# Holding decays, block-sum stores and row squares to the source's order, and loading x a step ahead, in a hybrid SSD and gated-linear-attention layer

## The chip, the cores and the metric

One core of one Trainium2 chip runs the kernel. The metric is the device time in microseconds of one execution. Three executions of the kernel before took 2349.11, 2349.48 and 2352.76 us; the median is 2349.48 us. Traces come from one further execution under the hardware profiler.

## The reference

One layer over 2048 tokens with 16 meta tokens in front, model width 1024, all in float32. `u` is the RMS-normed input; one projection of it gives the inputs of two branches, whose outputs are projected, gated and merged:

```python
def hybrid_layer(hres, norm_w, w_in, ...):
    u = rmsnorm(hres, norm_w)
    proj = jnp.einsum('bld,dn->bln', u, w_in)
    z, xbc, dt_raw, q, k, v, g_gla, a_lr, merge_g = split_cols(proj, IN_WIDTHS)
    xbc = jax.nn.silu(causal_depthwise_conv(xbc, conv_w, conv_b))
    ...
    y_m, s_m = ssd_chunked(xs[:, :m], dt[:, :m], a, bm[:, :m], cm[:, :m], N_META, s0)
    y_r, _ = ssd_chunked(xs[:, m:], dt[:, m:], a, bm[:, m:], cm[:, m:], SSD_CHUNK, s_m)
    ...
    o_r, _ = gla_chunked(q[:, m:], k[:, m:], v[:, m:], log_a[:, m:], GLA_CHUNK, st_m)
    ...
    branch_proj = jnp.einsum('blnc,ncd->blnd', branches, w_branch)
    gates = jax.nn.sigmoid(merge_g.reshape(b, l, N_BRANCH, D_MODEL))
    merged = jnp.sum(gates * branch_proj, axis=2)
    return hres + jnp.einsum('bld,de->ble', merged, w_out)
```

The final result is the RMS norm of this, without the meta rows. In the SSD branch `decay = exp(where(causal, seg, -inf))` with `seg` the differences of the running sums of `dt * a` in a chunk of 128 tokens; the meta tokens are a chunk of their own whose final state starts the first real chunk.

## The kernel before

**Two phases.** The first (to about 1557 us of the trace) does the norm, the input projection of both branches and the two scans; it leaves the branches' outputs and `u` in HBM. The second does the merge gates, the branch projections and the output projection as three kinds of stage with fast matrix multiplication (seven products in place of eight), whose sums of blocks of the right-hand side are needed beforehand. Every float32 product is three products of split operands: `accum` (L181) multiplies high by high (L183), high by low (L184) and low by high (L185).

**Blocks, groups, steps.** The first phase runs over four blocks of 512 tokens. A block has four SSD groups (`ssd_proj`, L448) and then four GLA heads (`gla_proj`, L602), the SSD half and the GLA half of the block. Each is a generator that yields after a *tile* of projection work: a group in the middle of and after its z tile and after each of four feature tiles (x, x, B, C); a head after q, k, the middle and the end of v and two gate tiles. That is six steps each. After every yield, `step()` (L813) moves every running background generator on by one piece, in the order in which they began: scans of earlier groups and heads (`ssd_scan`, `gla_scan`), the GLA gates (`gates`), the next block's `u` (`load_u` by way of `fetch_u`), and the block sums (`beside_unit`). So the source's order is tile, pieces of the others, tile, and so on.

**What is held to it.** TensorE's and SyncE's instructions are kept in source order (`manual_schedule` at L826). ScalarE, VectorE and GpSimd are ordered when the program is built, by a planner that takes an instruction as soon as it holds its inputs to be there; among those ready, the one earlier in the source comes first. So on these engines an instruction can stand far ahead of its place in the source. Once built, each engine runs its list in order and waits at each instruction until its inputs and buffers are there; this holds for DMA issues too, on SyncE (the sync queue) and on ScalarE.

**Buffers.** Weights land in "whl" (four buffers, two loads to a tile; `load_w` at L155). In block 0 they come as one float32 tile through "wr" (three buffers) and are split by ScalarE (L163) and GpSimd (L164), and the split pair is kept in HBM (L179); blocks 1 to 3 load the pair itself (L159). A feature tile's conv accumulator is in "acc" (two buffers, freed by L481), its result in "act" (eight). After the matmuls of a feature tile, ScalarE copies and scales it (L472, L473), VectorE adds three taps (L477), ScalarE takes a tanh (L480) and VectorE finishes silu (L481).

**Block sums.** `make_sums` (L72) runs for one unit in three steps: four loads into two "wr" buffers (L76); four subtractions on GpSimd (L80); two stores from ScalarE's queue (L83). `beside_unit` (L820) runs eight units one after the other, three steps each, so one run of eight fills one half of a block. It is begun at both halves of blocks 1 and 2 and at the first half of block 3: 40 units. The other units run in the second phase, from another pool.

**The next block's u.** `load_u` begins with the GLA half of the block before. For each of four chunks of 128 rows it loads the rows in two halves into "acc" (L256), squares and sums them on ScalarE (L257) and makes the reciprocal root; then TensorE spreads the roots (L278), and for each of eight column tiles of the transposed x it loads the tile into "acc" (L292), multiplies (L294), splits it (L296, L298) and stores it from ScalarE's queue (L297). Each chunk and each column is one step.

**The SSD scan.** `before(c)` transposes chunk c (L538), copies B (L547) and makes the decays: four Relu (L550) on `cb`, a broadcast row fetched by DMA (L490), one Exp (L552), times the masked scores (L553). `after(c)` multiplies (L562 to L565) and sums the squares of a row (L577). In block 0, `meta_state` (L513) multiplies and copies the meta tokens' state (L517), from which `after(0)` reads (L563).

**Late constants.** `late_constants` (L330) loads the gates' second weight and the masks; its first tile, `w2r`, is an "acc" buffer. It is called between block 0's first and second group.

Of the kernel before, what the change touches and what calls it, by code (L numbers as in the profile page):

```python
# [14 lines left out]
P = 128  # L15
# [25 lines left out]
def trunk_kernel(ctx: ExitStack, tc: tile.TileContext, xm, xmt, w_feat, w_tok, w_zm, w_br, w_o,  # L41
# [27 lines left out]
    UNIT = 2 * BLK  # L69
    nsb = seq // UNIT  # L70

    def make_sums(pool, tag, nb, braw, sums, j, c, store):  # L72
        cs = slice(c * HB, (c + 1) * HB)
        pair = [mk(pool, [P, 512], F32, tag, bufs=nb).rearrange("p (i c) -> p i c", i=2) for _ in range(2)]
        for r, (k, t) in zip((t[:, i] for t in pair for i in range(2)), ((0, 1), (0, 0), (1, 1), (1, 0))):
            nc.sync.dma_start(r, braw(4 * k + j, t)[:, cs])  # L76
        yield
        (b12, b11), (b22, b21) = [(t[:, 0], t[:, 1]) for t in pair]
        for o, x, y in ((b11, b12, b11), (b12, b22, b12), (b22, b22, b11), (b21, b21, b22)):
            nc.gpsimd.tensor_tensor(o, x, y, op=ALU.subtract)  # L80
        yield
        for dst, src in zip(sums, pair):
            store.dma_start(dst[j][:, :, cs], src)  # L83

    def new_sums(name):
        return [[wdram.tile([P, 2, BLK], F32, tag=f"{name}_t{i}_{j}", name=f"{name}_t{i}_{j}", bufs=1)
# [132 lines left out]
    def halves_of(pool, tag):  # L219

        bks = [bank(pool, tag) for _ in range(2)]
        return bks, [(i // 2, bks[i // 2][:, i % 2 * 256:(i % 2 + 1) * 256]) for i in range(4)]

    def rstd_of(ssq, n, scale):
        r = mk(sm, [P, 4], F32, "rstd")
        nc.vector.tensor_scalar(r[:, :n], ssq, scale, EPS, op0=ALU.mult, op1=ALU.add)
        nc.gpsimd.tensor_tensor(r[:, :n], r[:, :n], mhalf[:, :n], op=ALU.pow)
        return r
# [6 lines left out]
    def load_u(b):  # L235
        m0 = META if b == 0 else 0
        row0 = META - m0 + b * BLK
        tt = m0 + BLK
        pair = mk(upool, [P, 2, KT * (META + BLK)], F32R, "u")[:, :, :KT * tt]
        uh, ul = [pair[:, i].rearrange("p (k t) -> p k t", k=KT) for i in range(2)]  # L240

        def rows_rstd(r0, n, vector=False):
            ss = mk(sm, [P, 1], F32, "ss")
            if m0:
                xt = mk(wk, [P, D], F32, "tok4", bufs=NT4)
                nc.sync.dma_start(xt[:n], xm[r0:r0 + n, :])
                if vector:
                    nc.vector.scalar_tensor_tensor(xt[:n], xt[:n], 1.0, xt[:n], op0=ALU.mult, op1=ALU.mult,
                                                   accum_out=ss[:n])
                else:  # L250
                    nc.scalar.activation(xt[:n], xt[:n], AF.Square, accum_out=ss[:n])
            else:
                s2 = mk(sm, [P, 2], F32, "ss2")
                for i in range(2):
                    xt = mk(wk, [P, META + BLK], F32, "acc")[:, :BLK]
                    nc.sync.dma_start(xt, xm[r0:r0 + n, i * BLK:(i + 1) * BLK])  # L256
                    nc.scalar.activation(xt, xt, AF.Square, accum_out=s2[:, i:i + 1])  # L257
                nc.vector.tensor_tensor(ss, s2[:, 0:1], s2[:, 1:2], op=ALU.add)
            r = mk(sm, [P, 1], F32, "rs1")
            nc.vector.tensor_scalar(r[:n], ss[:n], 1.0 / D, EPS, op0=ALU.mult, op1=ALU.add)  # L260
            nc.gpsimd.tensor_tensor(r[:n], r[:n], mhalf[:n, 0:1], op=ALU.pow)
            return r

        rs = []
        if m0:
            rm_s = rows_rstd(0, META, True)
        for c in range(NCH):
            rs.append(rows_rstd(META + b * BLK + c * P, P, c % 2))
            yield
        if m0:  # L270
            rs.append(rm_s)
            nc.sync.dma_start(cst[:, :2], cf32[:, :2])
            nc.sync.dma_start(pv, pvec)
            for q in range(NWR):
                raws[f"zm_{q}"] = load_raw(w_zm[:, q * 288:(q + 1) * 288])
        rb = bank(pt, "pt")
        for c in range(NCH):
            nc.tensor.matmul(rb[:, c * P:(c + 1) * P], rs[c].to_broadcast([P, P]), ident, start=True, stop=True)  # L278
        rbs = [(rb, m0, BLK)]
        if m0:  # L280
            rm = bank(pt, "pt")
            nc.tensor.matmul(rm[:, :META], rs[NCH][:META].to_broadcast([META, P]), ident[:META, :META],
                             start=True, stop=True)
            rbs = [(rm, 0, META)] + rbs
        else:
            rbc = mk(wk, [P, 3 + META + BLK], F32, "cin")[:, :BLK]
            nc.scalar.activation(rbc, rb, AF.Copy)
            rbs = [(rbc, 0, BLK)]
            yield
        for kt in range(KT):  # L290
            xk = mk(wk, [P, META + BLK], F32, "act" if m0 else "acc", bufs=NACT if m0 else 2)[:, :tt]
            nc.sync.dma_start(xk, xmt[:, kt, row0:row0 + tt])  # L292
            for ps, a, n in rbs:
                nc.vector.scalar_tensor_tensor(xk[:, a:a + n], xk[:, a:a + n], norm_w[:, kt:kt + 1], ps[:, :n],  # L294
                                               op0=ALU.mult, op1=ALU.mult)
            nc.scalar.activation(uh[:, kt, :tt], xk, AF.Copy)  # L296
            nc.scalar.dma_start(u_left[b][kt], xk[:, m0:])  # L297
            nc.vector.tensor_tensor(ul[:, kt, :tt], xk, uh[:, kt, :tt].bitcast(F32), op=ALU.subtract)  # L298
            yield
        return uh, ul  # L300

# [26 lines left out]
    msk = const.tile([P, NMSK, P], U8, name="msk")  # L328

    def late_constants():  # L330
        w2r = mk(wk, [P, META + BLK], F32, "acc")[:48, :512]
        for i in range(3):
            nc.sync.dma_start(w2r[16 * i:16 * i + 16, :], gw2)
        nc.scalar.activation(w2, w2r, AF.Copy)
        nc.vector.tensor_tensor(w2[32:48], w2r[32:48], w2[32:48].bitcast(F32), op=ALU.subtract)
        mstg = mk(wk, [P, D], F32, "tok4", bufs=NT4)[:, :NMSK * P]
        nc.sync.dma_start(mstg, cmsk)
        nc.vector.tensor_copy(msk.rearrange("p l t -> p (l t)"), mstg)
# [153 lines left out]
    def ssd_scan(o, g, feats, zs):  # L492
# [37 lines left out]
        def before(c):  # L530
            a = m0 + c * P
            ci = ci0 + c
            if c + 1 < NCH:
                fetch_cb(o, g, c + 1)
            cb = cbs.pop((g, c))
            ps = bank(pt, "pt")
            for j, f in enumerate((x0, x1, bf)):
                nc.tensor.transpose(ps[:, j * P:(j + 1) * P], f[:, a:a + P], ident)  # L538
            px = ps[:, :256].rearrange("p (h c) -> p h c", c=64)
            xdt = mk(wk, [P, 4, 64], F32, "c1", bufs=NC1)  # L540
            nc.vector.tensor_tensor(xdt, px, hb(tkd[:, ci, hs], P), op=ALU.mult)
            xw = mk(wk, [P, 4, 64], F32, "c1", bufs=NC1)
            nc.vector.tensor_tensor(xw, px, hb(wde[:, ci, hs], P), op=ALU.mult)
            nc.vector.tensor_tensor(yt[:, c].rearrange("p (h c) -> p h c", c=64), px,
                                    hb(d_skip[:, hs], P), op=ALU.mult)
            bt = mk(wk, [P, P], F32, "bt")
            nc.scalar.activation(bt, ps[:, 256:384], AF.Copy)  # L547
            dm = mk(wk, [P, 4, P], F32, "sq", bufs=NSQ)
            for h in range(4):
                nc.scalar.activation(dm[:, h], cb[:, h], AF.Relu, scale=-1.0,  # L550
                                     bias=tkc[:, ci, 4 * g + h:4 * g + h + 1])
            nc.scalar.activation(dm, dm, AF.Exp, scale=-1.0)  # L552
            nc.vector.tensor_tensor(dm, dm, scm[:, c].unsqueeze(1).to_broadcast([P, 4, P]), op=ALU.mult)  # L553
            held[c] = xdt, xw, bt, dm

# [24 lines left out]
        yield  # L580
        if m0:
            meta_state()
        for c in range(1, NCH):
            before(c)
            after(c - 1)
            yield
# [233 lines left out]
    def beside_unit(key):  # L820
        for j in range(4):
            for c in range(2):
                yield from make_sums(wpool, "wr", NWR, *sums[key], j, c, nc.scalar)
                yield

    with tc.manual_schedule(engines={mybir.EngineType.PE, mybir.EngineType.SP}):  # L826
        for b in range(nblk):
            o = new_block(b, next_u[b])
            for i in range(SG + GH):
                if (b, i) in beside:  # L830
                    begin(beside_unit(beside[b, i]))
                if (b, i) == (0, 1):
                    late_constants()
                if i == 1:
                    begin(gates(o))
                if i == SG and b + 1 < nblk:
                    begin(fetch_u(b + 1))
                for _ in ssd_proj(o, i) if i < SG else gla_proj(o, i - SG):
                    step()
            save(0)  # L840
        while running or begun:
            step()
# [329 lines left out]
```

## Time and profile before

| | |
|---|---|
| median of three runs | 2349.48 us |
| the profiled execution | 2353.29 us |
| its span | 2351.5 us |
| mean granted TensorE clock | 0.982 |
| POOL wr L80 waiting for loads (wr<-y, wr<-u, wr<-in_w_o) | 172.7, 160.7, 68.8 us |
| SPq L159 waiting for PE pj L185 (weight buffers coming free) | 610.2 us, 188 times |

The span is the time from the first to the last instruction. PE is TensorE, PEld its weight loads, DVE VectorE, ACT ScalarE, POOL GpSimd, SP SyncE; SPq, ACTq and DVEq are the engines' instruction queues, in which DMA issues stand. L numbers are lines of the kernel before. In a row of waits, "PE pj L183 <- ACT whl L163: 10.1, 2, 6.7" reads: before the instruction at L183 that writes `pj`, PE was idle until ACT's L163 (writing `whl`) had ended, 10.1 us in total, twice, at most 6.7. In a timeline row the first number is the start, the second the duration (of a merged run, x and a count), and the bracket at the end the idle time before it and what ended it. In the list of DMA issues the last number is the median time in us from issue to landing.

### The profile page before, as it was taken

The numbers are of one execution on the slowest core, as the hardware profiler recorded it, in microseconds if no ns is written. First come the engines' busy times: TensorE is split into PE (matmuls) and PEld (weight loads), VectorE is DVE, ScalarE is ACT, GpSimd is POOL, SyncE is SP. The second block draws the span as 40 slices with busy tenths as digits, with TensorE's granted clock in tenths as the row PEclk, the third lists the DMA queues.
The fourth block names the chain that finished last, engine by engine and source line by source line (L and its number), as shares of the span: only waits on it lengthen the run. The fifth ranks groups of instructions, "written<-read, shape, count | busy, mean of one in ns | idle before, by whom it ended". The sixth has DMA issues, their size and how long they took to land.

```text
span 2351.5 us, 36473 instructions
## 1 busy us (share of the span) xinstructions
PE 2251.0 (96%) x12641; PEld 1962.2 (83%) x12641; DVE 1547.5 (66%) x2895; ACT 1181.6 (50%) x2758; POOL 672.9 (29%) x681
## 2 busy tenths in 40 slices
PE   7799999999999999999999999879999999999998
PEld 7689889889888988888988898768878788888786
DVE  5576665676675567566568655674578854778866
ACT  5565655465534455543456443464455454554543
POOL 4343433122321212221122200207423354423331
PEclk9899999999999999999999999989999999999999
DMA  7665875666786676777677654447577876777753
GB/s 270 225 206 184 299 252 193 204 218 223 240 274 191 205 223 219 238 258 224 194 225 221 205 174 157 154 135 254 194 242 261 297 236 203 251 272 252 254 165 122
DMA packets 301545, 518.05 MB, mean 220 GB/s; under 512 B 27696, under 2 KB 143664, under 8 KB 301360
## 3 DMA queue, kind: packets, MB, share of 16 engines
q1 hardware_dynamic: 200400, 402.84, 52.9%
q10 hardware_dynamic: 100960, 112.88, 13.8%
q8 instruction: 99, 1.62, 0.3%
q14 instruction: 86, 0.70, 0.1%
HBM read 368.42 MB, written 147.19 MB: 219 GB/s over the span
## 4 chain that ended last, share of the span: by engine, by line
PE 48%; DMA 6%; DVE 6%; ACT 3%; issue 2%; SPq 1%; POOL 1%; ACTq 0%; DVEq 0%; POOLq 0%
PE pj L183 6%; PE pj L185 6%; PE pj L184 6%; PE psa L183 4%; PE psa L185 4%; PE psa L184 4%; PE psb L184 2%; PE psb L185 2%; PE psb L183 2%; DVE b L893 1%; DMA br<-br_t 1%; PE psc L183 1%; PE psc L185 1%; PE psc L184 1%; PE pc L562 1%
## 5 line engine op out<-in xcount | busy, mean ns | idle before, releaser
L183 PE MATMUL pj<-u,whl 128*128 128x512 f32 (+1 forms) x1184 | 447.9, 378 | 10.5 <-ACT whl L163 3.5
L185 PE MATMUL pj<-u,whl 128*128 128x512 f32 (+1 forms) x1184 | 431.8, 365 | 0.8 <-POOL whl L164 0.8
L184 PE MATMUL pj<-u,whl 128*128 128x512 f32 (+1 forms) x1184 | 430.8, 364 | 0.0
L183 PE MATMUL pj<-whl,u 128*128 128x256 f32 (+1 forms) x992 | 290.3, 293 | 8.2 <-ACT whl L163 6.7
L185 PE MATMUL pj<-whl,u 128*128 128x256 f32 (+1 forms) x992 | 283.4, 286 | 1.5 <-DVE u L298 1.4
L184 PE MATMUL pj<-whl,u 128*128 128x256 f32 (+1 forms) x992 | 283.4, 286 | 1.0 <-POOL whl L164 1.0
L183 PEld LDWEIGHTS pj<-u,whl 128*128 128x128 f32 x1184 | 225.9, 191 | 48.8 <-ACT whl L163 3.9
L183 PE MATMUL psa<-b,a 128*128 128x512 f32 x640 | 249.8, 394 | 11.1 <-ACT sn L930 8.2
L185 PEld LDWEIGHTS pj<-u,whl 128*128 128x128 f32 x1184 | 224.9, 190 | 36.9 <-POOL whl L164 1.1
L184 PEld LDWEIGHTS pj<-u,whl 128*128 128x128 f32 x1184 | 225.5, 190 | 33.6
L185 PE MATMUL psa<-b,a 128*128 128x512 f32 x640 | 251.3, 393 | 1.2 <-DVE a L914 1.2
L184 PE MATMUL psa<-b,a 128*128 128x512 f32 x640 | 251.0, 392 | 0.0
L183 PEld LDWEIGHTS pj<-whl,u 128*128 128x128 f32 x992 | 191.2, 193 | 9.4 <-ACT whl L163 6.9
L184 PEld LDWEIGHTS pj<-whl,u 128*128 128x128 f32 x992 | 191.0, 193 | 2.1 <-POOL whl L164 1.6
L185 PEld LDWEIGHTS pj<-whl,u 128*128 128x128 f32 x992 | 190.8, 192 | 2.2 <-DVE u L298 2.2
L893 DVE TENSOR_TENSOR b<-br,b 128x512 fp32r<-128x512 f32 x196 | 153.1, 804 | 56.2 <-ACT b L892 55.7
L80 POOL TENSOR_TENSOR wr<-wr 128x256 f32<-128x256 f32 x80 | 65.1, 814 | 425.5 <-DMA wr<-y 169.7
L904 POOL TENSOR_TENSOR as<-ar,ar 128x512 f32<-128x512 f32 x40 | 57.8, 1446 | 447.5 <-DMA ar<-in_w_br 191.2
L164 POOL TENSOR_TENSOR whl<-wr,whl 128x512 fp32r<-128x512 f32 (+1 forms) x100 | 132.9, 1335 | 182.5 <-ACT whl L163 155.2
L892 ACT ACTIVATE b<-br 128x512 fp32r<-128x512 f32 x196 | 119.2, 626 | 112.3 <-DMA br<-br_t 41.5
L914 DVE TENSOR_TENSOR a<-ar,a 128x512 fp32r<-128x512 f32 x160 | 131.8, 839 | 64.4 <-ACT a L913 64.1
L477 DVE SCALAR_TENSOR_TENSOR acc<-cin,hcw,acc 128x512 f32<-128x512 f32 (+1 forms) x192 | 154.6, 805 | 27.0 <-ACT acc L473 26.3
(271 smaller groups left out, 5062.7 us busy)
## 6 DMA issues: line engine op xcount, KB each, us to landing
whl<-k_s SPq DMA_DIRECT2D x96, 512.0 KB, 4.5
whl<-k_g SPq DMA_DIRECT2D x96, 512.0 KB, 4.2
whl<-k_v SPq DMA_DIRECT2D x48, 512.0 KB, 3.7
whl<-k_z SPq DMA_DIRECT2D x36, 512.0 KB, 3.8
wr<-in_w_feat SPq DMA_DIRECT2D x64, 256.0 KB, 4.2
k_s<-whl SPq DMA_DIRECT2D x32, 512.0 KB, 3.7
cb<-cumd ACTq DMA_DIRECT2D x64, 256.0 KB, 5.4
y<-gg ACTq DMA_DIRECT2D x64, 256.0 KB, 4.5
```

Of the source, the lines that this page charges most:

```text
L80: nc.gpsimd.tensor_tensor(o, x, y, op=ALU.subtract)
L164: nc.gpsimd.tensor_tensor(hl[:, 1], raw, hl[:, 0].bitcast(F32), op=ALU.subtract)
L183: nc.tensor.matmul(ps, sh, mh, start=first, stop=False, **kw)
L184: nc.tensor.matmul(ps, sh, ml, start=False, stop=False, **kw)
L185: nc.tensor.matmul(ps, sl, mh, start=False, stop=last, **kw)
L477: nc.vector.scalar_tensor_tensor(acc, cin[:, k:k + tt], hcw[:, ti, k:k + 1], acc, op0=ALU.mult, op1=ALU.add)
L562: nc.tensor.matmul(py[:, h * 64:(h + 1) * 64], dm[:, h], xdt[:, h], start=True, stop=True)
L892: nc.scalar.activation(t[:, 0], raw, AF.Copy)
L893: nc.vector.tensor_tensor(t[:, 1], raw, t[:, 0].bitcast(F32), op=ALU.subtract)
L904: nc.gpsimd.tensor_tensor(s1, a21, a22, op=ALU.add)
L914: nc.vector.tensor_tensor(t[:, 1], src, t[:, 0].bitcast(F32), op=ALU.subtract)
```

## The change

- `make_sums` takes a function `order`; in the first phase it is `tc.keep_in_program_order`, which ties an instruction, in the built order alone and without a wait, behind the instruction that precedes it on its engine in the source. The 80 stores of L83 in the first phase, the decays (L550, L552) and the row squares of blocks 1 to 3 (L257) are so tied. What is tied can no longer be put ahead of that one instruction.
- The two halves of a chunk's rows are both allocated and loaded, then comes a step, then both are squared. This makes four more steps in `load_u` for blocks 1 to 3.
- A column of x is loaded in the step before the one that multiplies it, by a function `column`; for blocks 1 to 3 one more step lies ahead of the first.
- `w2r` of the late constants is an "act" buffer, and the call moves to block 0's first group, behind the second half of its z tile.
- In block 0 a step lies between `meta_state` and the next chunk.

```diff
-    def make_sums(pool, tag, nb, braw, sums, j, c, store):
+    def make_sums(pool, tag, nb, braw, sums, j, c, store, order=lambda ins: ins):
...
         for dst, src in zip(sums, pair):
-            store.dma_start(dst[j][:, :, cs], src)
+            order(store.dma_start(dst[j][:, :, cs], src))
...
+    in_order = tc.keep_in_program_order
...
                 s2 = mk(sm, [P, 2], F32, "ss2")
-                for i in range(2):
-                    xt = mk(wk, [P, META + BLK], F32, "acc")[:, :BLK]
+                xts = [mk(wk, [P, META + BLK], F32, "acc")[:, :BLK] for _ in range(2)]
+                for i, xt in enumerate(xts):
                     nc.sync.dma_start(xt, xm[r0:r0 + n, i * BLK:(i + 1) * BLK])
-                    nc.scalar.activation(xt, xt, AF.Square, accum_out=s2[:, i:i + 1])
+                yield
+                for i, xt in enumerate(xts):
+                    in_order(nc.scalar.activation(xt, xt, AF.Square, accum_out=s2[:, i:i + 1]))
...
-            rm_s = rows_rstd(0, META, True)
+            rm_s = yield from rows_rstd(0, META, True)
         for c in range(NCH):
-            rs.append(rows_rstd(META + b * BLK + c * P, P, c % 2))
+            r = yield from rows_rstd(META + b * BLK + c * P, P, c % 2)
+            rs.append(r)
             yield
...
-        for kt in range(KT):
+        def column(kt):
             xk = mk(wk, [P, META + BLK], F32, "act" if m0 else "acc", bufs=NACT if m0 else 2)[:, :tt]
             nc.sync.dma_start(xk, xmt[:, kt, row0:row0 + tt])
+            return xk
+
+        xk = column(0)
+        if not m0:
+            yield
+        for kt in range(KT):
...
             nc.vector.tensor_tensor(ul[:, kt, :tt], xk, uh[:, kt, :tt].bitcast(F32), op=ALU.subtract)
+            if kt + 1 < KT:
+                xk = column(kt + 1)
             yield
...
     def late_constants():
-        w2r = mk(wk, [P, META + BLK], F32, "acc")[:48, :512]
+        w2r = mk(wk, [P, META + BLK], F32, "act", bufs=NACT)[:48, :512]
...
             for h in range(4):
-                nc.scalar.activation(dm[:, h], cb[:, h], AF.Relu, scale=-1.0,
-                                     bias=tkc[:, ci, 4 * g + h:4 * g + h + 1])
-            nc.scalar.activation(dm, dm, AF.Exp, scale=-1.0)
+                in_order(nc.scalar.activation(dm[:, h], cb[:, h], AF.Relu, scale=-1.0,
+                                              bias=tkc[:, ci, 4 * g + h:4 * g + h + 1]))
+            in_order(nc.scalar.activation(dm, dm, AF.Exp, scale=-1.0))
...
         if m0:
             meta_state()
+            yield
...
-                yield from make_sums(wpool, "wr", NWR, *sums[key], j, c, nc.scalar)
+                yield from make_sums(wpool, "wr", NWR, *sums[key], j, c, nc.scalar, in_order)
                 yield
...
-                if (b, i) == (0, 1):
-                    late_constants()
...
-                for _ in ssd_proj(o, i) if i < SG else gla_proj(o, i - SG):
+                for n, _ in enumerate(ssd_proj(o, i) if i < SG else gla_proj(o, i - SG)):
                     step()
+                    if (b, i, n) == (0, 0, 1):
+                        late_constants()
```

## The prediction

> **What bounds the kernel now.** I read the page first (totals), then the busy time by stage, then PE's waits, then the granted clock beside the longest of them.
>
> ```profile
> span 2351.5 us, 36473 instructions
> PE 2251.0 (96%) x12641; PEld 1962.2 (83%) x12641; DVE 1547.5 (66%) x2895; ACT 1181.6 (50%) x2758; POOL 672.9 (29%) x681
> ```
> ```profile
> 0.00:420.00 420.00, 377.35 (x2654) 351.38 (x2655) 264.80 (x516) 236.10 (x595) 161.75 (x151) 0.97 0.68 232
> 420.00:1510.00 1090.00, 1072.94 (x6499) 953.82 (x6498) 690.30 (x1528) 537.02 (x1385) 206.23 (x289) 0.99 0.67 215
> ```
>
> The windows' columns are the stretch, then busy time (instructions) of PE, PEld, DVE, ACT, POOL, then granted clock, DMA share, GB/s. TensorE is the bound. The first phase, which the change touches, runs to about 1510 us: block 0 (first row) leaves PE 43 us idle, blocks 1 to 3 (second row) only 17 us. No rearrangement of other engines can win more than that idle time and the slow clock behind it; anything that makes PE wait for weights is lost in full.
>
> PE's waits in these two stretches (total, times, longest):
>
> ```profile
> PE pj L183 <- ACT whl L163: 10.1, 2, 6.7
> PE pc L563 <- DVE s_ssd L517: 5.3, 1, 5.3
> PE pj L183 <- ACT g_all L435: 3.3, 2, 3.1
> PE pj L184 <- POOL whl L164: 1.0, 2, 0.8
> ...
> PE pc L562 <- DVE sq L553: 5.4, 3, 3.0
> PE pj L183 <- DMA whl<-k_g: 2.5, 2, 1.5
> ```
>
> A wait costs more than its idle time. Windows just behind four of them:
>
> ```profile
> 64.00:71.00 7.00, 3.53 (x13) 2.95 (x14) 1.39 (x3) 2.63 (x5) 2.89 (x3) 0.56 1.00 384
> 88.00:92.00 4.00, 4.00 (x21) 4.00 (x22) 1.47 (x3) 3.25 (x10) 0.00 (x0) 0.58 0.83 289
> 98.00:105.00 7.00, 2.54 (x8) 2.19 (x9) 6.76 (x19) 2.90 (x9) 2.48 (x3) 0.57 0.70 226
> 638.00:642.00 4.00, 4.00 (x20) 3.79 (x19) 3.07 (x8) 2.44 (x9) 1.47 (x2) 0.57 0.92 350
> ```
>
> The clock (third number from the end) falls to 0.56 to 0.58. Lost clock is window times (1 minus clock): 3.1 us behind the 6.7 us wait, 3.0 behind the 5.3, 1.7 behind the 3.1 and the 3.0.
>
> **The parts that take something away.** *Late constants.* In the source these loads stand between block 0's first and second group, and their first tile waits for an "acc" buffer:
>
> ```profile
> SPq L333 <- DVE act L481: 15.6, 1, 15.6
> ...
> 41.94 0.42 SPq L173 DMA_DIRECT2D wr<-in_w_feat  x1
> 58.64 1.25 SPq L333 DMA_DIRECT2D acc<-in_gw  x3
> ...
> 66.42 0.58 PE L183 MATMUL pj<-whl,u 128*128 128x256 f32 x1 [6.66 <-ACT whl L163]
> ```
>
> The sync queue issues nothing from 42.4 to 58.6; the next group's weights stand behind, and PE idles 6.7 us plus 0.8 for the low half. Moved to an "act" buffer and ahead of the group's first feature tile, the wait goes: 6.7 + 0.8 + 3.1 of clock, less at most 1.7 us for their four issues (1.25 + 0.42) now in front of that tile's weights: **-8.9**. These rows also show the rule on which the rest turns: the sync queue is in source order, and what blocks it for long reaches PE as late weights.
>
> *Decays.* Held behind the copy in front of them, four sets (L550, L552) no longer fill ScalarE ahead of the gates' L435 in block 0 (3.1 + 1.7 of clock) nor, with the squares of x that wait on their loads, ahead of L553's inputs in blocks 1 and 2 (5.4 for three waits, 1.7 for each of the two long ones): **-4.8 and -8.8**. Each set now runs one step before its matmuls, 7.6 us (560.36 to 567.93 in PE's rows below), and PE works on a feature tile meanwhile, so I add nothing for lateness. If that cover does not suffice, the nearest row is the same 3.0 us wait.
>
> *Meta state.* One feature tile now lies between the meta matmul and the first reader of its copy (L517 to L563): 5.3 + 3.0 of clock, **-8.3**.
>
> *Row squares and columns of x.* Row loads now take both "acc" buffers at once, so at each block's GLA half the second waits for the last feature tile's L481 instead of a square, and stands ahead of the key tile's weights. The 2.5 us on whl<-k_g therefore stays; I take 0, between -2.5 (gone) and +5 (as much again for each of two). A column's load moves a step up, yet needs the buffer whose store now left one step, not two, before:
>
> ```profile
> SPq L292 <- DMA u<-acc: 28.7, 8, 6.3
> ```
>
> Its buffers, not its place, set the pace (two in a ring), and the multiplication may still be placed as early as before. I take 0, between -2.5 again and +28.7, if these queue waits doubled and all reached PE.
>
> Together about **-31**.
>
> **The part that adds: the held stores.** Forty units make block sums beside blocks 1 to 3, in three steps: four loads (L76), subtractions, two stores (L83). "wr" has three buffers and a unit takes two, so the third load of the next unit waits until this unit's first store has landed. In the source that load comes one step behind the store.
>
> ```profile
> L83 ACTq DMA_DIRECT2D gate_t<-wr x32: 520/521/562, 611.3 to 1324.6; - x32
> L83 ACTq DMA_DIRECT2D br_t<-wr x32: 520/521/559, 802.0 to 1139.8; - x32
> L83 ACTq DMA_DIRECT2D out_t<-wr x16: 520/521/607, 434.2 to 592.0; - x16
> ...
> DMA to landing us min/median/max: 2.4/4.7/7.6
> ```
>
> Now the store is issued as soon as the subtractions end, far ahead of its place, and ScalarE sometimes waits for them there:
>
> ```profile
> ACT sq L552 <- POOL wr L80: 12.4, 7, 2.6
> ```
>
> Held, it goes out only behind the ScalarE instruction before it in the source, mostly the tanh L480 of the tile of that step. How the three queues stand (last group of block 1; sync queue, ScalarE, PE):
>
> ```profile
> 560.96 1.81 SPq L76 DMA_DIRECT2D wr<-in_w_o  x4
> 565.40 3.05 SPq L159 DMA_DIRECT2D whl<-k_z  x2
> 574.90 6.80 SPq L159 DMA_DIRECT2D whl<-k_s  x4
> 581.75 2.54 SPq L76 DMA_DIRECT2D wr<-in_w_o  x4
> 586.25 3.03 SPq L159 DMA_DIRECT2D whl<-k_s  x2
> ...
> 565.01 0.63 ACT L480 ACTIVATE act<-acc 128x512 f32<-128x512 f32 x1 [2.67 <-DVE acc L477]
> 567.54 0.53 ACTq L83 DMA_DIRECT2D out_t<-wr  x1
> 574.13 0.63 ACT L480 ACTIVATE act<-acc 128x512 f32<-128x512 f32 x1 [3.14 <-DVE acc L477]
> 597.23 0.63 ACT L480 ACTIVATE act<-acc 128x512 f32<-128x512 f32 x1 [0.15 <-DVE acc L477]
> ...
> 560.36 0.49 PE L538 MATMUL pt<-cst,act 128*128 128x128 f32 x3
> 567.93 1.00 PE L562 MATMUL pc<-c,sq 128*128 128x64 f32 x8
> 575.43 0.28 PE L183 MATMUL pj<-whl,u 128*128 128x256 f32 x1
> 589.09 1.00 PE L562 MATMUL pc<-c,sq 128*128 128x64 f32 x8
> 598.23 0.58 PE L183 MATMUL pj<-u,whl 128*128 128x512 f32 x1
> ```
>
> The sync queue runs two tiles ahead of PE. At 581.75 it issues the loads of the step behind the group's *second* feature tile, while PE begins the *first*, which ends before 589.09. The store that these loads follow went out at 567.54. Held, it waits for that first tile's tanh, which ends at 597.86. So the third load, and the weights issued at 586.25, would wait for 597.86 and a store's landing, while PE wants those weights at 598.23. ScalarE's own later work is hardly queued by this; the sync queue's is.
>
> Per unit, counted from the tile's last matmul. The tanh ends 5.3 us later (560.36 to 565.64), 6.8 (567.93 to 574.76) or 8.8 (589.09 to 597.86). I take 6.0, near the low end, because a PE that stalls gives VectorE and ScalarE time to catch up. Add 4.7 for the store, 0.9 for the two loads left (1.81 for four), and the weights' landing:
>
> ```profile
> whl<-k_z SPq DMA_DIRECT2D x36, 512.0 KB, 3.8
> whl<-k_s SPq DMA_DIRECT2D x96, 512.0 KB, 4.5
> ```
>
> Behind a group's fourth tile: 6.0 + 4.7 + 0.9 + 3.8 = 15.4, wanted after 7.5 (567.93 to 575.43): stall **7.9**. Behind its first tile: 16.1 with 4.5, wanted after 9.1 (589.09 to 598.23): stall **7.0**. By the source order, of the 24 units in the SSD halves 8 are of the first kind and 6 of the second; 3 stand behind an attention split of the scan before; 6 behind something that is done early; the last has no successor. Of the 16 in the GLA halves, 4 stand behind the last SSD scan's row square (L577); in the others what stands ahead is early, or a 96-matmul value tile gives the queue time. I price the 3 and the 4 at half, 4 each, between 0 and 9. Sum: 8 x 7.9 + 6 x 7.0 + 7 x 4 = 133. Each of these 21 stalls is as long as the waits above, so each brings 1.7 to 3.1 of slow clock; 2.4 x 21 = 50. **+183.**
>
> The Trainium skill ("TensorE: Matmul & The Clock Gate", Part 1: The HAM clock gate) says that an idle window of about 3.4 us halves the clock until one busy window has passed, and that for modelling the ramp is under 1% of a typical span. The 0.56 to 0.58 above agree with the halving; by the 1% (an estimate, some 23 us) the 50 would be less than half and the sum about 27 us lower. I keep the rows: here the stalls come every third tile.
>
> Total: -31 + 183 = **+152** on the profiled execution's own 2353.3 us (span 2351.5 and 1.8 around it). That execution was 3.8 above the median of 2349.48, so the median becomes about **2501**.
>
> Bounds: low, tanh at 5.3, store 2.4, the seven at nothing, clock 1.7 for 14 stalls: 8 x 4.9 + 6 x 4.0 + 24 = 87, net +56, 2405. High, tanh at 8.8, the seven at 9, clock 3.1 for 21: 8 x 10.7 + 6 x 9.8 + 63 + 65 = 272, with +5 and +28.7 for x and the -31: +275, 2625.
>
> **The rivals.**
> *The stores' delay never reaches the queue* (faster). If ScalarE reaches the store before the sync queue reaches the third load, only the -31 is left: **2319**. For it: today's queue shows no wait on these buffers at all. Against: that is because stores leave 30 us before their place; with them held, the queue would have to lose 15 us of lead (third load at about 582.7, the tanh's end at 597.86). It decides for "faster" if the stalls come to less than 31 us, or 1.5 per unit of the 21.
>
> *The holding does not bind* (faster). It ties each instruction to the one before it alone; were that one placed early too, stores and decays would stay where they are, and only late constants and meta state would pay: -17, **2332**. For it: 6 of the 24 are such cases. Against: L480 needs its own tile's matmuls.
>
> *The sync queue is held at x as well* (slower still). Squares behind late ScalarE work hold the next rows, columns hold on their stores, each ahead of weights; the +28.7 and +5 on top: **2535**. For it: 28.7 us of such waits already. Against: steps in the GLA halves are longer than in the SSD halves.
>
> **How the numbers follow.** Forecast 0.70, the first rival 0.12, the second 0.05, the third 0.10, and 0.03 for gain and loss that cancel. A measurement of this kernel tells about 0.2% (4.7 us) from no change. So faster 0.17, same 0.03, slower 0.80. The forecast's own range is 2405 to 2625. The range given, 2345 to 2615, leaves out the faster rivals and a tail above.
>
> **What would show it.** The sync queue waiting at L76 for sums<-wr, some 10 to 20 us each time in the SSD halves; PE waiting on whl<-k_s and whl<-k_z, which have no such row now; L83 issued just behind L480; the clock at half behind each; PE's idle time between 420 and 1510 up from 17 to over 100 us. Right in the rest: no L333 wait, no 5.3 on L563, no 3.0 on L562, no squares waiting on in_xm. If L76 shows no wait on the stores, the forecast is wrong in its main term.

## The result, and the profile after

The changed kernel takes **2509.48 us** (median of five runs, 2502.12 to 2512.68) against 2349.48 before (five runs, 2345.52 to 2352.76): ratio **1.067**, 95% interval 1.065 to 1.070. Slower, as forecast, by 160 us where +152 was predicted. The lines of the code have moved: L258 loads rows of x, L261 squares them, L297 loads a column; L493 is the tanh (L480 before), L485 and L486 the copy and the scaling ahead of it (L472, L473), L551 the transposition (L538), L560 the copy of B (L547), L563, L565 and L566 the decays (L550, L552, L553), L575 the product that reads them (L562).

The page after, and the busy time by stage (columns as before):

```profile
span 2507.2 us, 36394 instructions
PE 2298.8 (92%) x12641; PEld 1995.6 (80%) x12641; DVE 1542.5 (62%) x2895; ACT 1193.4 (48%) x2758; POOL 671.4 (27%) x681
```
```profile
420.00:1510.00 1090.00, 974.10 (x5646) 855.52 (x5645) 606.21 (x1346) 487.54 (x1226) 200.74 (x285) 0.94 0.59 194
```

The span grew by 155.7 us. PE runs the same 12641 products; its busy time grew by 47.8 (a lower clock) and the rest, 107.9, is idle time. In the stretch that the prediction named PE now idles 116 us (1090 less 974.10), before 17.

The sync queue's waits and PE's (total, times, longest):

```profile
SPq L76 <- DMA br_t<-wr: 134.0, 12, 20.8
SPq L76 <- DMA gate_t<-wr: 119.9, 11, 20.8
SPq L76 <- DMA out_t<-wr: 93.7, 7, 22.3
SPq L258 <- ACT acc L261: 92.5, 14, 16.8
```
```profile
PE pj L183 <- DMA whl<-k_z: 42.1, 7, 9.0
PE pj L183 <- DMA whl<-k_g: 38.3, 6, 9.9
PE pj L183 <- DMA whl<-k_s: 16.9, 6, 3.8
PE pj L183 <- ACT whl L163: 16.9, 5, 5.4
PE pc L575 <- DVE sq L566: 12.0, 9, 2.4
```

The first three rows of the sync queue are new: 30 waits of 11.6 us on average for a held store. So are PE's rows for k_z and k_s. The fourth row of the queue and PE's wait on L163 are the part that the prediction had as a rival; the last row is one that it had at nothing.

One stall in the timeline after (start, duration; sync queue, ScalarE, PE):

```profile
573.00 15.15 SPq L76 DMA_DIRECT2D wr<-in_w_o  x4
588.25 1.79 SPq L159 DMA_DIRECT2D whl<-k_s  x4
...
584.62 0.64 ACT L493 ACTIVATE act<-acc 128x512 f32<-128x512 f32 x1 [0.84 <-DVE acc L490]
584.68 1.20 ACTq L83 DMA_DIRECT2D out_t<-wr  x2
...
579.97 0.49 PE L551 MATMUL pt<-cst,act 128*128 128x128 f32 x3
592.16 0.50 PE L183 MATMUL pj<-u,whl 128*128 128x512 f32 x1 [2.37 <-DMA whl<-k_s]
```

Behind the tile's last product the transposition starts at 579.97, its tanh starts at 584.62, and the store is issued just behind the tanh. The four loads of the next unit, which took the queue 2.54 us before, hold it for 15.15, until the store has landed. Only then do the weights leave, and PE waits for them.

### The profile page after: what moved, and what is told of

The parts are those of the page before. It is cut to its first block, busy times and chain, and to the rows that moved or that the text cites. A ratio compares the mean times of both kernels' runs of the same rounds, so it can differ in the third digit from the quotient of the medians.

```text
span 2507.2 us, 36394 instructions
## 1 busy us (share of the span) xinstructions
PE 2298.8 (92%) x12641; PEld 1995.6 (80%) x12641; DVE 1542.5 (62%) x2895; ACT 1193.4 (48%) x2758; POOL 671.4 (27%) x681
## 5 line engine op out<-in xcount | busy, mean ns | idle before, releaser
L183 PE MATMUL pj<-u,whl 128*128 128x512 f32 (+1 forms) x1184 | 459.1, 388 | 75.9 <-DMA whl<-k_g 38.3
L185 PE MATMUL pj<-u,whl 128*128 128x512 f32 (+1 forms) x1184 | 443.1, 374 | 2.4 <-POOL whl L164 1.5
L184 PE MATMUL pj<-u,whl 128*128 128x512 f32 (+1 forms) x1184 | 442.6, 374 | 0.0
L183 PE MATMUL pj<-whl,u 128*128 128x256 f32 (+1 forms) x992 | 299.6, 302 | 53.8 <-DMA whl<-k_z 42.1
L183 PEld LDWEIGHTS pj<-u,whl 128*128 128x128 f32 x1184 | 233.9, 198 | 121.9 <-DMA whl<-k_g 41.1
L184 PE MATMUL pj<-whl,u 128*128 128x256 f32 (+1 forms) x992 | 290.2, 293 | 1.8 <-POOL whl L164 1.8
L185 PE MATMUL pj<-whl,u 128*128 128x256 f32 (+1 forms) x992 | 289.7, 292 | 1.5 <-DVE u L309 1.4
L185 PEld LDWEIGHTS pj<-u,whl 128*128 128x128 f32 x1184 | 233.0, 197 | 41.6 <-POOL whl L164 3.8
L184 PEld LDWEIGHTS pj<-u,whl 128*128 128x128 f32 x1184 | 234.0, 198 | 35.0
L183 PE MATMUL psa<-b,a 128*128 128x512 f32 x640 | 249.5, 394 | 12.3 <-ACT sn L944 9.1
L183 PEld LDWEIGHTS pj<-whl,u 128*128 128x128 f32 x992 | 198.1, 200 | 59.7 <-DMA whl<-k_z 44.4
L184 PEld LDWEIGHTS pj<-whl,u 128*128 128x128 f32 x992 | 198.5, 200 | 2.7 <-POOL whl L164 2.3
L185 PEld LDWEIGHTS pj<-whl,u 128*128 128x128 f32 x992 | 197.8, 199 | 2.2 <-DVE u L309 2.2
```

Of the source, the lines that this page charges most:

```text
L183: nc.tensor.matmul(ps, sh, mh, start=first, stop=False, **kw)
L184: nc.tensor.matmul(ps, sh, ml, start=False, stop=False, **kw)
L185: nc.tensor.matmul(ps, sl, mh, start=False, stop=last, **kw)
```

## The experiments

Twelve kernels; each ratio is against further runs of the kernel before on the same chip, whose medians were 2350 to 2354.

**The stores, taken out or alone.** *stores_free* is the whole change, the stores not held; *stores_only* is the kernel before with nothing but the stores held.

```diff
-                yield from make_sums(wpool, "wr", NWR, *sums[key], j, c, nc.scalar, in_order)
+                yield from make_sums(wpool, "wr", NWR, *sums[key], j, c, nc.scalar)
```

> The changed kernel with the block-sum stores no longer held; decays, row squares, the loads a step ahead and the moved parts stay. By head and group the changed kernel lost 97 us in the SSD halves of blocks 1 to 3 and about 69 us in the first two GLA heads of blocks 0 to 2, and won 12 us in block 0's SSD half. Theory A (the held stores block the sync queue in the SSD halves; block 0's GLA half has no block sums, so the GLA loss is that of the x loads): about 2410 us, no wait of L76 on stores left, the GLA loss unchanged. Rival B (the stores cost both halves, block 0's GLA loss is something else): about 2370 us. Rival C (late decays make the SSD loss): still about 2510 us.

Measured: 2407.14 us, ratio 1.0235 (1.021 to 1.0259).

> The kernel before with the block-sum stores held and nothing else. Theory A: +97 us in the SSD halves and little in the GLA halves, about 2445 us, with waits of L76 on the stores' landing of 10 to 20 us each. Rival B: +97 and some 40 in the GLA halves, about 2490 us. Rival C: about 2350 us.

Measured: 2528.37 us, ratio 1.0742 (1.072 to 1.0764). Slower alone than in company: +179 here, +102 (2509 - 2407) as the last edit of the whole. The first was as theory A had it; the second was above all three, by 83 above A (2445) and by 38 above the nearest (B, 2490).

*after_wr4* holds the stores and gives "wr" a fourth buffer (three small tiles get two buffers to make room):

```diff
-NWR = 3
+NWR = 4
...
-            for q in range(NWR):
+            for q in range(3):
```

> The changed kernel with four wr buffers in place of three (three raw tiles still loaded ahead; three small tiles of one to four columns have two buffers in place of four to make room). The stores stay held, but a unit's third load no longer needs the buffer of the store one step before. If the loss goes through that buffer: the same as with the stores free, about 2410 us (theory A) or 2370 us (rival B), though the stores stand behind L493 as before. If the loss is in the position of the stores on ScalarE itself: about 2510 us.

Measured: 2423.74 us, ratio 1.0295 (1.0265 to 1.0326). The busy time by stage of this kernel:

```profile
420.00:1510.00 1090.00, 1035.12 (x6150) 914.62 (x6149) 666.99 (x1459) 520.03 (x1319) 216.60 (x290) 0.97 0.65 207
```

PE's idle time there is 55 us, not 116. Nothing is different but buffers, the stores go out as late as in the change, and 86 of the 102 us are gone. Nearly all of that lies in the SSD halves. Measured from the first projection product of a half to that of the next, those of blocks 1 to 3 take 191.1, 188.0 and 189.1 us, as in stores_free (191.8, 188.8, 188.1), where the change takes 219.9, 214.4 and 217.7. There, what costs is the load that waits for a buffer of the held store, not the store's lateness as such. The GLA halves of blocks 1 and 2 keep the change's length (201.9 and 202.3 against 201.8 and 200.9; stores_free 189.5 and 193.5). There the sync queue stands at the next rows of x instead, 120.9 us in 17 waits for the squares over the kernel, 99.6 in 14 in stores_free; in block 1 it stands until 699.85 for squares that start at 699.10, behind held stores issued at 697.86 and 698.42. So in the GLA halves a late store seems to cost through the square placed behind it; no run tries that by itself.

*early_parts* is the kernel before with decays held, late constants and meta state moved (x and stores as before):

> The kernel before with the parts that take something away alone: decays held, late constants moved to an act buffer and earlier, meta state apart; stores, squares and x loads as before. By the prediction -8.9, -8.3, -4.8 and -8.8: about 2320 us. If decays that run in their place come late (the changed kernel waits 12.0 us on L566 in nine waits, the kernel before 5.4): 2335 to 2350 us.

Measured: 2354.67 us, ratio 1.0014 (0.9993 to 1.0035). No gain, where -31 had been predicted. So stores_free, which adds only the x edits to it, says that these cost 52. Two terms of the prediction needed an explanation: the -31 for the parts that take something away, and the 0 for the x edits.

**The x edits.** All three are stores_free with one part undone.

*x_free_squares* holds the squares no longer:

```diff
-                    in_order(nc.scalar.activation(xt, xt, AF.Square, accum_out=s2[:, i:i + 1]))
+                    nc.scalar.activation(xt, xt, AF.Square, accum_out=s2[:, i:i + 1])
```

> The whole change without the holding of the stores, and with the row squares no longer held either: rows still loaded a step before they are squared, columns still one product ahead. Measured with the squares held: 2407; with no x edits at all: 2355, so the x edits are worth about 52. Theory X1 (the held square sits behind the half group's other work on ScalarE, so that its buffer comes free late and the sync queue stands at the next row load: the row of the sync queue waiting at L258 on the square is 99.6 us in 14 with the stores free, 26.0 in 15 without the x edits): the loss goes, 2350 to 2365, and the row at L258 falls to about 30. Theory X2 (the two buffers of the columns, now filled one ahead, hold the queue): no change, 2400 to 2410. Theory X3 (two row buffers asked for in one step, with the square a step later, cost the wait whether the square is held or not): 2395 to 2410.

Measured: 2352.39 us, ratio 1.0002 (0.9987 to 1.0018).

*rows_back* loads and squares one half after the other in one step, as before:

```diff
-                xts = [mk(wk, [P, META + BLK], F32, "acc")[:, :BLK] for _ in range(2)]
-                for i, xt in enumerate(xts):
+                for i in range(2):
+                    xt = mk(wk, [P, META + BLK], F32, "acc")[:, :BLK]
                     nc.sync.dma_start(xt, xm[r0:r0 + n, i * BLK:(i + 1) * BLK])
-                yield
-                for i, xt in enumerate(xts):
-                    in_order(nc.scalar.activation(xt, xt, AF.Square, accum_out=s2[:, i:i + 1]))
+                    nc.scalar.activation(xt, xt, AF.Square, accum_out=s2[:, i:i + 1])
```

> The whole change without the holding of the stores, and with rows loaded and squared as before (one half after the other, in one step, not held); columns still loaded one product ahead. X1 (held squares): 2350 to 2365. X2 (columns ahead): 2400 to 2410. X3 (two row buffers in one step): 2350 to 2365. With the run before, X1 and X3 are told apart.

Measured: 2350.82 us, ratio 1.0011 (0.9994 to 1.0028).

*cols_back* loads each column in the step that uses it:

```diff
-        xk = column(0)
-        if not m0:
-            yield
         for kt in range(KT):
+            xk = column(kt)
...
-            if kt + 1 < KT:
-                xk = column(kt + 1)
```

> The whole change without the holding of the stores, and with each column of x loaded in the step that uses it, as before; rows still loaded a step ahead with held squares. X1 (held squares) and X3 (two row buffers in one step): no change, 2400 to 2410, with the sync queue's wait at the row load still near 100 us. X2 (columns ahead): 2350 to 2365.

Measured: 2406.31 us, ratio 1.0235 (1.0207 to 1.0264). All three as X1 said: the loss is the holding of the squares, and loading ahead is innocent. Every kernel with held squares has held decays too, so what the squares would cost behind free decays was not measured. The sync queue's row in stores_free and in x_free_squares:

```profile
SPq L258 <- ACT acc L261: 99.6, 14, 16.4
```
```profile
SPq L258 <- ACT acc L261: 12.1, 3, 5.1
```

How it happens, in block 0's GLA half of stores_free (sync queue, ScalarE, PE):

```profile
231.78 0.33 SPq L173 DMA_DIRECT2D wr<-in_w_tok  x1
245.46 0.94 SPq L258 DMA_DIRECT2D acc<-in_xm  x2
246.92 0.42 SPq L173 DMA_DIRECT2D wr<-in_w_tok  x1
...
242.71 0.28 ACT L560 ACTIVATE bt<-pt 128x128 f32<-128x128 f32 x1 [1.96 <-DVE tok L557]
244.19 0.63 ACT L565 ACTIVATE sq<-sq 128x512 f32<-128x512 f32 x1
244.72 0.61 ACT L261 ACTIVATE acc<-acc 128x512 f32<-128x512 f32 x1
...
252.34 0.38 PE L183 MATMUL pj<-whl,u 128*128 128x256 f32 x1 [2.50 <-ACT whl L163]
```

and the first chunk's two squares, with the load of the next rows, in x_free_squares:

```profile
230.41 1.27 SPq L258 DMA_DIRECT2D acc<-in_xm  x2
...
219.88 0.63 ACT L261 ACTIVATE acc<-acc 128x512 f32<-128x512 f32 x1
225.47 0.63 ACT L261 ACTIVATE acc<-acc 128x512 f32<-128x512 f32 x1 [2.85 <-DMA acc<-in_xm]
```

Free, the squares run as soon as their rows land, at 219.88 and 225.47. Held, they stand behind a copy of B (which waits for VectorE) and the decays, and run from 244.72 on. The buffer that a square frees is the one that the next rows want; their load stands in the sync queue ahead of weights, and the queue issues nothing for 13 us (232.11 to 245.46). It is the stores' mechanism again, with another buffer.

**The moves and the decays.** *moves_only* is early_parts without the held decays; *decays_only* is the kernel before with only the decays held; *none_held* is the change with nothing held (moves and x loads ahead).

```diff
             for h in range(4):
-                nc.scalar.activation(dm[:, h], cb[:, h], AF.Relu, scale=-1.0,
-                                     bias=tkc[:, ci, 4 * g + h:4 * g + h + 1])
-            nc.scalar.activation(dm, dm, AF.Exp, scale=-1.0)
+                tc.keep_in_program_order(nc.scalar.activation(dm[:, h], cb[:, h], AF.Relu, scale=-1.0,
+                                                              bias=tkc[:, ci, 4 * g + h:4 * g + h + 1]))
+            tc.keep_in_program_order(nc.scalar.activation(dm, dm, AF.Exp, scale=-1.0))
```

That diff is all of decays_only; in moves_only and none_held the decays are as in its removed lines.

> The kernel before with the late constants moved to the second step and their buffer changed, and the yield behind the meta state; decays, stores, squares and x as before. With the decays held as well this was 2355, with the SSD half of block 0 shorter by 13.7 and those of blocks 1 to 3 longer by 8.6, 4.9 and 2.3. Theory D (the held decays cost those 16 and the moves alone earn the 13.7): 2333 to 2340, and the SSD halves of blocks 1 to 3 at 185.0, 184.1 and 185.3 as in the kernel before. Theory E (the held decays earned part of the 13.7 in block 0, as my prediction had it with 4.8): 2340 to 2347. No gain (2349) if block 0's halves only moved the wait.

Measured: 2335.35 us, ratio 0.9933 (0.9912 to 0.9955).

> The kernel before with the decays alone held. Moves and held decays gave 2355, the moves alone 2335. Theory D (held decays cost, whatever stands beside them): 2349.5 + 19, or 2362 to 2372, with the SSD halves of blocks 1 to 3 longer by 16 in all and the product of the decayed scores waiting more often on its left operand. The prediction had -13.6 for this edit: 2336. If the cost comes only with the moves: 2345 to 2353.

Measured: 2367.48 us, ratio 1.007 (1.0046 to 1.0094).

> The change with nothing held to its place: late constants and meta state moved, rows and columns of x loaded ahead, stores, decays and squares free. With the moves alone: 2335. If loading x ahead is worth nothing once the squares are free: 2332 to 2339. If it spares the queue's remaining waits at rows and columns (about 25 us of the sync queue, none of it a wait of PE): up to 5 less, 2328 to 2333. If two rows at once hold the queue: 2340 to 2350.

Measured: 2333.58 us, ratio 0.992 (0.9901 to 0.994). As theory D had it: the moves earn 14, the held decays cost about 18. moves_only and none_held are the fastest of the study and can't be told apart, so loading x ahead is worth nothing measurable.

One late set of decays in decays_only (this kernel has the line numbers of before; VectorE, ScalarE, PE):

```profile
516.75 0.41 DVE L544 TENSOR_TENSOR tok<-pt,pv 128x256 f32<-128x256 f32 x1
519.73 0.69 DVE L553 TENSOR_TENSOR sq<-sq,sq 128x512 f32<-128x512 f32 x1
...
517.26 0.28 ACT L547 ACTIVATE bt<-pt 128x128 f32<-128x128 f32 x1 [2.57 <-DVE tok L544]
517.43 1.27 ACT L550 ACTIVATE sq<-cb,tkc 128x128 f32<-128x128 f32 x4
518.74 0.63 ACT L552 ACTIVATE sq<-sq 128x512 f32<-128x512 f32 x1
...
510.65 0.49 PE L538 MATMUL pt<-cst,act 128*128 128x128 f32 x3
520.47 0.77 PE L562 MATMUL pc<-c,sq 128*128 128x64 f32 x5 [1.76 <-DVE sq L553]
```

**Two or more held together.** *after_free_squares* is the whole change with the edit of x_free_squares; *stores_moves_x* has the decays free as well (the removed lines of the last diff), so that the stores alone are held.

> The whole change with the row squares alone not held: stores and decays held, late constants and meta state moved, x loaded ahead. The held squares cost 55 (2407 against 2352) where the stores were free, the held stores 102 (2509 against 2407) where the squares were held, and 179 (2528) alone. Theory F (two stalls of one sync queue in different halves of a block, that add: the stores' in the SSD halves, the squares' in the GLA halves): 2509 - 55, or 2450 to 2465. Theory G (each stall of the queue in the GLA halves also delays what the other would have delayed, so that one hides most of the other): 2500 to 2530, with the GLA halves of blocks 1 and 2 still near 201 for the held stores, as they are with the held stores alone.

Measured: 2466.26 us, ratio 1.0488 (1.046 to 1.0516). Nearly theory F (2450 to 2465): the squares cost 43 beside held stores, against 55 without. But the held stores cost 114 here (2466 - 2352), not 179.

> The change with the stores alone held, on top of the moves and the x loads: decays and squares free. The held stores cost 179 alone (2528 - 2349), but 114 with the decays held, the moves made and x loaded ahead (2466 - 2352). Theory H (the held decays ease what the held stores cost: ScalarE reaches the held store sooner, or does other work at another time): without them 2466 rises, 2490 to 2520, the moves having taken 14 off 2528. Theory I (the moves and the x loads ahead ease it, as the first GLA head of blocks 1 and 2 says, 65 us with the stores alone and 55 in the run with everything but the squares): the held decays cost their own 18 here as well, and the time is 2440 to 2455. A time between says that both do part.

Measured: 2502.13 us, ratio 1.0629 (1.06 to 1.0657). Theory H: the held decays, which cost 18 alone, *save* 36 once the stores are held. PE's wait on the tile behind the held store in stores_moves_x and in after_free_squares:

```profile
PE pj L183 <- DMA whl<-k_s: 31.9, 6, 5.9
```
```profile
PE pj L183 <- DMA whl<-k_s: 17.4, 6, 3.4
```

ScalarE and PE around one such tile in stores_moves_x, decays free:

```profile
614.04 1.28 ACT L563 ACTIVATE sq<-cb,tkc 128x128 f32<-128x128 f32 x4 [0.65 <-DMA cb<-cumd]
615.23 0.57 ACT L485 ACTIVATE cin<-pj 128x512 f32<-128x512 f32 x1
620.39 0.63 ACT L493 ACTIVATE act<-acc 128x512 f32<-128x512 f32 x1 [0.15 <-DVE acc L490]
...
613.24 0.49 PE L551 MATMUL pt<-cst,act 128*128 128x128 f32 x3
```

and in after_free_squares, decays held:

```profile
608.77 0.60 ACT L485 ACTIVATE cin<-pj 128x512 f32<-128x512 f32 x1 [1.92 <-PE pj L185]
...
613.23 0.63 ACT L493 ACTIVATE act<-acc 128x512 f32<-128x512 f32 x1 [0.84 <-DVE acc L490]
...
608.57 0.49 PE L551 MATMUL pt<-cst,act 128*128 128x128 f32 x3
```

From the tile's last product (the start of L551) to its tanh: 7.2 us with the decays free, 4.7 with them held. The other tiles with a store just behind their tanh agree: 4.7 to 5.1 in six of after_free_squares, 7.1 in four of stores_moves_x. In the rows shown free decays are taken as soon as their broadcast rows land, in front of the tile's own copy L485. The copy comes 1.8 us later by it (2.0 behind the product against 0.2), and the tanh with the store tied behind it 2.5. That concerns the SSD halves, which are 28 us shorter in all with the decays held; the GLA halves of blocks 1 and 2 are 13 us shorter as well, and no row here shows why.

## Why the prediction was right, and where by luck

Adding the edits one after the other, with the prediction's terms beside them:

| step | kernel | us | measured | predicted |
|---|---|---|---|---|
| nothing | before | 2349.5 | | |
| moves, x loaded ahead | none_held | 2333.6 | -16 | -17.2 + 0 |
| decays held | x_free_squares | 2352.4 | +19 | -13.6 |
| stores held | after_free_squares | 2466.3 | +114 | +183 |
| squares held | after | 2509.5 | +43 | 0 |

The kernel before lay at 2350 to 2354 beside these runs, so a single step is good to some 5 us. The sum is +160 against +152, but three terms are off by +33, -69 and +43, and they cancel. The direction and the main mechanism were shown; the closeness of 2501 to 2509 was not earned.

**Held stores: right in mechanism; the price is near that of the edit alone, and this in part by luck.** Waits at L76 for the stores, PE's new rows, L83 just behind the tanh, the clock and the idle time came as listed, and a fourth buffer takes away the part in the SSD halves. Alone the edit costs 179 where 183 stood. The page of stores_only:

```profile
span 2527.3 us, 36459 instructions
PE 2303.4 (91%) x12641; PEld 1998.1 (79%) x12641; DVE 1550.2 (61%) x2895; ACT 1184.8 (47%) x2758; POOL 681.8 (27%) x681
```

Against before, its PE is busy 52.4 us longer (predicted 50 of slow clock) and idle 123.4 longer (predicted 133). The rows behind the idle time:

```profile
PE pj L183 <- DMA whl<-k_z: 43.9, 11, 8.5
PE pj L183 <- DMA whl<-k_g: 42.2, 6, 8.6
PE pj L183 <- DMA whl<-k_s: 32.7, 6, 7.5
PE pc L562 <- DVE s_ssd L568: 12.4, 3, 4.7
```

In the SSD halves the prediction had stalls of 117 us (8 x 7.9 + 6 x 7.0 + 3 x 4); the rows for k_z and k_s have 77. In the GLA halves it had 16 (4 x 4); k_g has 42, with 2.5 before. The last row (0.4 before) it did not have at all. By length, the SSD halves of blocks 1 to 3 grew by 128 us in all, where the prediction's stalls and their clock make 158 (117 and 17 times 2.4), and the GLA halves of blocks 1 and 2 by 41, where they make 26 (16 and 4 times 2.4). So the stalls behind feature tiles were priced too high, those of the GLA halves too low, and the two errors cancel in part.

In the whole change the failed step is that the stall per unit was worked out from the order of before and then added to the other edits. With the decays held the tanh no longer waits behind other decays, and the stall shrinks. In the timeline after, the chain is 5.3 us from the tile's last product to the tanh's end (579.97 to 585.26; 6.0 taken), 2.9 to the last of the loads' issues (588.15; 4.7 + 0.9 taken) and 4.0 to PE's product (4.5 taken): 12.2 in place of 16.1, a stall of 2.4 in place of 7.0. The store's landing was the largest error there; the store is also issued at 584.68, ahead of the tanh's end, where the prediction let it go out behind that end. The list of instructions of L83 after:

```profile
L83 ACTq DMA_DIRECT2D out_t<-wr x16: 521/556/632, 451.0 to 668.7; - x16
...
DMA to landing us min/median/max: 2.4/2.7/9.4
```

Its median is 2.7, not the 4.7 of before; the low bound had 2.4.

**Decays: the wrong sign.** The failed step is "PE works on a feature tile meanwhile, so I add nothing for lateness". The waits that the prediction wanted to win back did not go: in decays_only PE's wait on the gates' L435 is 3.7 us (3.3 before) and that on L553 8.8 in six (5.4 in three before). And the step of 7.6 us that was to cover them is mostly used up before ScalarE may begin. What the decays are tied to is the copy of B, and that copy waits for VectorE (43.4 us in 34 waits in decays_only, 18.0 in 27 before): in the rows of decays_only the transposition starts at 510.65, VectorE reaches L544 at 516.75, the copy starts at 517.26, and 3.2 us of copy, decays and L553 follow, to 520.42; PE stands idle from 518.71. The prediction checked that ScalarE has time, not when the instruction it tied them to is ready. The wait is 1.76 us there; over the kernel (x_free_squares) it is

```profile
PE pc L575 <- DVE sq L566: 12.7, 9, 2.4
```

where none_held has 0.3 in one wait. Between the profiled executions of these two, 20.7 us apart, PE is idle 8.4 us longer in all, since other waits shrank, and busy 12.3 longer, at a clock of 0.981 against 0.986. In decays_only the row grows by 3.4 alone, and two others grow with it, PE's wait on ScalarE's L591 (9.2, before 2.9) and on VectorE's L787 (10.2, before 5.6). That the held decays cost 18 is measured; that late decays are the whole of it is not shown.

**Squares: a rival, priced low and given 0.10.** "Squares behind late ScalarE work hold the next rows" is what happened; the prediction instead let the second row load wait for the last feature tile and took 0, with +34 as its upper end for all x edits. It is +43 with the stores held and +55 without. That rival's counter-argument, longer steps in the GLA halves, does not hold in block 0, where ScalarE and GpSimd also split the weights: measured from the first projection product of the half to that of the next, block 0's GLA half grows from 201.1 (after_free_squares) to 227.9 us (after), those of blocks 1 and 2 by 10.3 and 8.0. The other half of the same rival, columns held on their stores, is refuted by cols_back.

**Late constants and meta state: right.** -17.2 predicted, -14 measured (the ratio's interval is -10.6 to -20.7 us). In moves_only the sync queue's wait at L333 and PE's at L563 for L517 have no row any more, and PE's first row of before, 10.1 us in two waits, reads

```profile
PE pj L183 <- ACT whl L163: 1.6, 1, 1.6
```

**The first two rivals fell**: the stores' delay does reach the queue, and the holding binds.

## What to carry to other kernels

Before an instruction is tied to its place, look at what stands just ahead of it in the source, when *that* is ready, and which buffer waits for the tied one; the price is paid by whichever in-order queue has an instruction waiting for that buffer, here the sync queue with the weights behind it. A tie costs most where the buffers run out: a fourth buffer gave back 86 us of the 102, nearly all of it in the SSD halves; in the GLA halves, where the queue then stood for the squares' buffers, it gave back nothing. Prices of several such edits don't add, since each moves the instructions that another is tied to, so a forecast for a bundle needs the order after the other edits, and a sum that comes out right proves no term.

## What the runs showed of the hardware

Stalls that recur cost clock again. Behind PE's 7.46 us of idle time at 556.75 to 564.21 in the changed kernel:

```profile
564.00:570.00 6.00, 5.79 (x28) 5.79 (x29) 0.00 (x0) 0.27 (x1) 0.00 (x0) 0.54 0.53 213
```

The clock is 0.54 there; behind the wait of 2.37 us in the stall shown first it is 0.68 between 592 and 596. Over the whole of stores_only PE is busy 52 us longer for the same products, 2.1% of the span. The Trainium skill ("TensorE: Matmul & The Clock Gate", Part 1: The HAM clock gate) puts the ramp, which it describes at the start of a kernel, at under 1% of a typical span for modelling. That figure does not fit a kernel whose stalls come every few tiles, and the trace decides.

The stores land faster when the sync queue stands still for them: 2.7 us in place of 4.7, while the transfers' share between 420 and 1510 us falls from 0.67 to 0.59. Being held is not what does it. In after_wr4 they are held as well, but the queue does not wait for them, the share is 0.65, and their median is 5.0; in the four kernels where it does wait it is 2.6 or 2.7. That the stores find emptier transfer engines fits all of these.
